# Fewer and larger transfers in the attention phase of a hybrid encoder layer

## The chip, the cores and the metric

The kernel runs on one core of one Trainium2 chip. The metric is the device time of one execution in microseconds (us). The kernel before was timed three times: 2056.21, 2058.32 and 2059.30 us, median 2058.32. About 0.2% (4 us) is what a measurement of this kernel can tell from no change.

## The reference

One layer over a prompt of 2048 frames and a sample of 32 new frames, width 1024, all in float32. One input projection gives, for every frame, q, k, v and a gate z of an attention branch A, q, k, v, a gate z and two small vectors of a delta-rule branch B, and two gates of 1024 columns each:

```python
qa, ka, va, za, qkv_b, zb, a_b, b_b, gate_a, gate_b = split_projection(x @ w_in)
oa = chunk_band_attention(qa, ka, va, rel_bias)        # 8 heads x 64, 9-chunk band of keys
ya = (oa.reshape(bsz, t, A_WIDTH) * jax.nn.silu(za)) @ w_branch_a
...                                                     # conv, gated delta rule in chunks of 64 -> ob
yb = (ob * jax.nn.silu(zb)) @ w_branch_b
mix = jax.nn.sigmoid(gate_a) * ya + jax.nn.sigmoid(gate_b) * yb
y = layer_norm(ALPHA * x + mix @ w_out, ln_g, ln_b)
```

The sample attends to 512 cached keys and values and to itself. Besides y, the layer returns the newest 512 rows of k and v, the last rows before the convolution and the final states.

## The kernel before

**Stages.** The 2048 frames are done in two halves of 1024 columns (the second with the 32 sample columns). For each half there is a branch-B stage and then a branch-A stage: B of half 0, A of half 0, B of half 1, A of half 1. A last stage, the merge, does the two branch products, the gates, the output product and the layer norm in eight blocks of 256 columns. Under all four stages one stream of projection jobs runs on PE (`multiply`, tile `pj` in PSUM, two banks): a job is a weight of 128 columns, split into an f16 high part `whi` and low part `wlo`, times the split input `hi`, `lo`, in column blocks of 512 or 272. Each finished product is read out of its bank by an `evac` stream, which then gives the bank back.

**Branch A.** The eight heads are four pairs `p`, two heads of 64 channels on the 128 partitions. For a pair, four jobs give v, k, q and z. K and Q are split into f16 parts too (`divide_rows`, line 1513) and must lie in layouts of their own: `kst` holds for head h its high part on its own 64 partitions and its low part on the other 64; `qd` holds the high part of head h on both halves; `ql` holds the low part on its own half, zeros on the other. So `divide_rows` writes both parts into a staging tile `part`, and DMAs carry 64-partition pieces from there into `kst`, `qd` and `ql` (lines 1683 and 1733). V's two parts go through `part` as well, and two transposing DMAs per 512 columns turn them into `vt` (line 1617). The scores of a tile of 128 queries are two products into `a`, then bias and maximum on DVE, the exponential on ACT, a split into `pu`, a transposing DMA into `pt`, and 15 products into `c` (line 1882). `store` (line 1907) fetches 64 KB of the gate z from DRAM into `ga`, transposes the result `ob` on PE, multiplies, and writes 64 KB of the gated result `g` back to DRAM. In half 1 the last 512 rows of k also leave through `kr` (line 1674, two buffers): an ACT read of the `pj` bank, PE transposes, ACT copies, DMAs to the output.

**Early products.** During A of half 1, branch B's results are already there, so its branch products (weights and `g` each in a high and a low part) are done early, as filling for PE (`early_g`, `early_sg`, `early`, line 2178 on): for each block of 256 columns and each of 8 row groups, 12 products into a `b` bank, a gate value tile `sge` loaded from DRAM, one DVE operation, a store of `sge` to DRAM. The g loads of successive blocks alternate between two places. The merge then loads these tiles again as `sg`.

**Order.** All of it is written by generators. A planner (`Flow`) gives each instruction and each DMA an assumed cost, and the stream with the earliest assumed clock emits next. The order in which instructions are emitted is then the fixed order of each engine's queue. Nearly all DMAs are issued from one queue, that of SyncE (SP): line 290 for plain ones, line 301 for transposing ones. An engine whose next instruction must wait holds up what stands behind it. `yield t` in a stream means "plan the next instruction not before t", where t is the assumed landing; `MARGIN` (1.6 us), `SLACK` (2.5 us) and `LEAD` are added to or taken from it.

Of the kernel before, what the change touches and what calls it, by code (L numbers as in the profile page):

```python
# [275 lines left out]
def trunk(ctx: ExitStack, tc: tile.TileContext, x_p, x_s, cache_k, cache_v, st_conv, st_gdn,  # L276
# [382 lines left out]

    def divide():  # L660

        while True:
# [8 lines left out]
            yield t  # L671
# [826 lines left out]
    def phase_a(half):  # L1498
# [8 lines left out]
        bias_slots, vs_slot, sample_slot = [gate(2), gate(1)], gate(2), gate(1)  # L1507
# [5 lines left out]
        def divide_rows(ps, m, leave):  # L1513

            i = yield from part_slots.take()
            hi, lo = parts[i][:, 0], parts[i][:, 1]
            S.activation(out=hi[:, 0:m], in_=ps[:, 0:m], func=AF.Copy, scale=SMALL)
            yield
            V.scalar_tensor_tensor(out=lo[:, 0:m], in0=ps[:, 0:m], scalar=SMALL, in1=hi[:, 0:m],
                                   op0=ALU.mult, op1=ALU.subtract)  # L1520
            yield from leave()
            return hi, lo, i
# [62 lines left out]
        def job_v(k):  # L1585
# [3 lines left out]
            def begin():  # L1589
                nonlocal vf, vt, t0  # L1590
                vf = ap.tile([P, KW + DEC], F32, tag="vf", bufs=1, name=f"vf{p}")
                k.vt = vt = ap.tile([P, 2, KW // P, P], F16, tag="vt", bufs=2, name=f"vt{p}")
                t0 = dma(vf[:, 0:BAND], v_dram[p][:]) if last else 0.0

            def rest():
# [10 lines left out]
                for t in range(0, KW // P, 4):  # L1606
# [45 lines left out]
        def job_k(k):  # L1652
# [10 lines left out]
            def evac(bi, c0, n, gcol, ps):  # L1663
# [36 lines left out]
        def job_q(k):  # L1700
# [18 lines left out]
            def evac(bi, c0, n, gcol, ps):  # L1719
# [18 lines left out]
                part_slots.back(place)  # L1738
# [52 lines left out]
        def scores():  # L1791
            before = mark()
            before.done()
            for k in pairs:
                for t in range(8 + SKEW):
                    for h, i in ((0, t), (1, t - SKEW)):
# [5 lines left out]
                        if h == 0:  # L1802
                            w = k.tiles[i] = Tile()
                            w.rs = sums[:, i + k.p % 2 * 8, :]
                            w.og, w.done = None, 0
# [60 lines left out]
        def product(h, k, t, gt, w, pu, place, nk, kc, at):  # L1866
# [12 lines left out]
            for i in range(nk):  # L1879
                kt = kc // P + i  # L1880
                oc = w.ps[:, h * HD:(h + 1) * HD]
                PE.matmul(oc, pt_[:, i], vt[:, 0, kt, hr], start=(i == 0), stop=False)
                PE.matmul(oc, pt_[:, i], vt[:, 1, kt, hr], start=False, stop=False)
                PE.matmul(oc, pt_[:, nk + i], vt[:, 0, kt, hr], start=False, stop=(i == nk - 1))
# [18 lines left out]
        NGA = 3  # L1903
# [649 lines left out]
```

## Time and profile before

| | us |
|---|---|
| median of three runs | 2058.32 |
| the profiled execution's own time | 2060.79 |
| its span, first to last instruction | 2059.0 |
| PE busy | 1920.5 (93%) |
| DVE busy | 1394.3 (68%) |
| ACT busy | 970.5 (47%) |
| GpSimd (POOL) busy | 806.0 (39%) |

The mean granted TensorE clock was 0.971. The page shows one execution. A busy PE is not PE at its peak: matmuls are pipelined, and a recorded matmul contains the wait for the one ahead of it. In the trace B of half 0 reaches to about 496 us, A of half 0 to about 815, B of half 1 to about 1280, A of half 1 to about 1735; the merge is in its steady form from about 1785 and the last block ends from 2014 on.

### The profile page before, as it was taken

The page shows a single profiled execution, that of the slowest core. Times are in us where ns is not written, and L with a number is a line of the kernel's source. Part 1 is how long each engine was busy: PE and PEld are TensorE (multiplying, and loading weights), DVE is VectorE, ACT ScalarE, POOL GpSimd, SP SyncE. Part 2 cuts the span into 40 slices and gives each one's busy share as a digit, 9 for nine tenths or more (in the row PEclk, how much of TensorE's full clock was granted, in tenths as well). Part 3 has the DMA queues.
Part 4 walks back from the last instruction along what each step waited for, and adds up shares of the span by engine and source line. Part 5 has one row for each costly group of instructions (what it writes and reads, how often), then busy time and mean ns, then how long its engine had stood idle before and what let it go on. Part 6 is the DMA issues. An engine that isn't in the chain of part 4 may idle for free.

```text
span 2059.0 us, 41305 instructions
## 1 busy us (share of the span) xinstructions
PE 1920.5 (93%) x14513; PEld 1350.5 (66%) x14513; DVE 1394.3 (68%) x4498; ACT 970.5 (47%) x1982; POOL 806.0 (39%) x1139
## 2 busy tenths in 40 slices
PE   8999999999998989999999999899998987799997
PEld 5455676665444556676777777577676765688885
DVE  7789989852457658589889884364454545675766
ACT  6655546444655766664445433454454544311110
POOL 7443334433333335344333423322221212455664
PEclk9999999999998999999999999999999998899998
DMA  3224232432577785223232333687778768634442
GB/s 139 65 76 125 74 98 66 112 91 95 135 183 170 173 190 136 76 71 96 68 86 65 98 95 91 163 200 162 182 164 207 168 167 200 212 125 152 143 132 76
DMA packets 398233, 263.91 MB, mean 128 GB/s; under 512 B 252994, under 2 KB 346542, under 8 KB 398024
## 3 DMA queue, kind: packets, MB, share of 16 engines
q1 hardware_dynamic: 398024, 261.26, 48.5%
q8 instruction: 114, 1.87, 0.4%
q14 instruction: 95, 0.78, 0.1%
HBM read 148.63 MB, written 63.24 MB: 103 GB/s over the span
## 4 chain that ended last, share of the span: by engine, by line
PE 59%; DVE 17%; DMA 6%; issue 6%; POOL 5%; ACT 4%; SPq 2%; POOLq 0%; DVEq 0%; ACTq 0%
PE pj L267 32%; PE b L267 13%; PE a L267 7%; PE x L267 3%; DVE acc L267 2%; DVE sys_t L267 2%; DVE sys_u L267 2%; POOL wlo L267 2%; PE c L267 2%; SPq L290 2%; PE o L267 2%; DMA pt<-pu 1%; DMA glo<-g 1%; DVE kd_bd L267 1%; ACT wraw L267 1%
## 5 line engine op out<-in xcount | busy, mean ns | idle before, releaser
L267 PE MATMUL pj<-hi,whi 128*128 128x512 f16 (+2 forms) x1992 | 649.8, 341 | 19.2 <-ACT whi L267 4.8
L267 PE MATMUL pj<-hi,wlo 128*128 128x512 f16 (+2 forms) x1952 | 641.5, 342 | 0.8 <-POOL wlo L267 0.7
L267 PEld LDWEIGHTS <-whi 128*128 128x128 f16 x3984 | 411.2, 105 | 232.6 <-issue 13.6
L267 PE MATMUL pj<-lo,whi 128*128 128x512 f16 (+2 forms) x1992 | 458.9, 340 | 0.0
L267 POOL TENSOR_TENSOR wlo<-wraw,whi 128x256 f16<-128x256 f32 x384 | 268.5, 722 | 441.6 <-ACT whi L267 334.5
L267 PEld LDWEIGHTS <-wlo 128*128 128x128 f16 x1952 | 206.3, 106 | 129.6 <-issue 20.4
L267 POOL TENSOR_TENSOR pu<-sb,pu 128x640 f16<-128x640 f32 (+2 forms) x64 | 82.7, 1292 | 208.8 <-ACT pu L267 177.9
L267 ACT ACTIVATE wraw<-wraw,w_scale 128x1024 f32<-128x1024 f32 (+1 forms) x98 | 111.4, 1137 | 90.7 <-DVE w_scale L267 80.1
L267 ACT ACTIVATE sb<-sb,mx,unit 128x640 f32<-128x640 f32 (+4 forms) x128 | 108.7, 850 | 83.4 <-DVE mx L267 80.0
L267 ACT CAST whi<-wraw 128x512 f16<-128x512 f32 (+1 forms) x196 | 119.0, 610 | 35.8 <-PE pj L267 33.0
L267 DVE TENSOR_TENSOR sys_u<-sys_u,sys_t 128x60 f32<-128x60 f32 (+24 forms) x527 | 124.8, 243 | 5.7
L267 ACT CAST mh<-sg 128x256 fp32r<-128x256 f32 x64 | 25.7, 406 | 210.5 <-DVE sg L267 187.7
L267 DVE SCALAR_TENSOR_TENSOR acc<-raw,cwT,acc 128x512 f32<-128x512 f32 x144 | 112.7, 783 | 7.9 <-ACT acc L267 6.5
L267 DVE TENSOR_TENSOR sys_t<-sys_u,sys_p 128x60 f32<-128x60 f32 (+21 forms) x459 | 109.9, 242 | 5.5
L267 POOL TENSOR_TENSOR w_scale<-w_scale,mhalf 128x1 f32<-128x1 f32 x49 | 30.6, 624 | 177.6 <-DVE w_scale L267 134.6
L267 DVE CUSTOM_DVE_ANT_0 sb<-a,bias 128x320 f32<-128x320 f32 (+5 forms) x136 | 66.2, 498 | 49.1 <-PE a L267 46.8
L267 PEld LDWEIGHTS <-pt 128*128 128x128 f16 x1680 | 66.7, 99 | 44.0 <-DMA pt<-pu 24.0
L267 ACT COPY v_t<-o 128x64 f32<-128x64 f32 x132 | 27.7, 210 | 142.8 <-PE o L267 99.5
L267 PE MATMUL c<-vt,pt 128*128 128x64 f16 x1680 | 72.1, 195 | 20.7 <-DMA pt<-pu 13.9
L267 DVE SCALAR_TENSOR_TENSOR sge<-sge,b 128x256 f32<-128x256 f32 (+1 forms) x64 | 27.1, 423 | 92.3 <-DMA sge<-sig 44.9
L267 ACT CAST pu<-sb 128x640 f16<-128x640 f32 (+4 forms) x128 | 81.9, 650 | 6.6 <-DMA pt<-pu 6.3
L267 ACT ACTIVATE sig<-pj,w_half 128x512 f32<-128x512 f32 (+2 forms) x84 | 49.3, 587 | 71.3 <-PE pj L267 63.6
(351 smaller groups left out, 4323.0 us busy)
## 6 DMA issues: line engine op xcount, KB each, us to landing
wraw<-in_w_in SPq DMA_DIRECT2D x192, 256.0 KB
sg<-sig SPq DMA_DIRECT2D x112, 128.0 KB
sig<-sig SPq DMA_DIRECT2D x44, 256.0 KB
sys_p<-sol_p SPq DMA_DIRECT2D x68, 128.0 KB
x<-in_x_p SPq DMA_DIRECT2D x16, 512.0 KB
xt<-in_x_p SPq DMA_DIRECT2D x16, 512.0 KB
out_y_p<-xt SPq DMA_DIRECT2D x16, 512.0 KB
glo<-g SPq DMA_DIRECT2D x14, 512.0 KB
```

What stands on the lines that cost most here:

```text
L267: r = f(*a, **k)
L290: eng.dma_start(dst, src)
```

## The change

- K and Q are split per head, straight out of PSUM: ACT writes the high part into its place in `kst` or `qd` (64 partitions at a time, so two instructions instead of one), DVE writes the low part of Q into `ql`, that of K into `part`. What is left for DMAs is K's low part, and a copy of Q's high part to the other half: 2 issues per block instead of 4 (K) and 6 (Q).
- V's two parts are turned by one transposing DMA instead of two, with a matching layout of `vt`.
- The gate is applied per two row tiles: loads and stores of 256 columns, one DVE operation; two places of two tiles instead of three of one.
- The early products of two 256-column blocks share one PSUM bank, one gate tile of 512 columns, one DVE operation, one load and one store (three such pairs; the last two blocks stay single). The products themselves stay 256 columns wide. A pair takes both places of the g loads. The gate tiles of early products and merge come from one pool of three, and the merge begins its loads when the early stream has ended.
- `kr` has one buffer instead of two.
- The planner assumes later landings: for weights (from the sixth job on), for the cached keys of the sample, for the early gate tiles (by 1.6 us ahead of the products, by 2.5 us ahead of the DVE operation).

The core of the diff:

```diff
-            yield t
+            yield t + (SLACK if len(started) > 4 else 0.0)
+            started.append(job)
...
-        bias_slots, vs_slot, sample_slot = [gate(2), gate(1)], gate(2), gate(1)
+        bias_slots, vs_slot, sample_slot = [gate(2), gate(1)], gate(1), gate(1)
...
-        def divide_rows(ps, m, leave):
-            i = yield from part_slots.take()
-            hi, lo = parts[i][:, 0], parts[i][:, 1]
-            S.activation(out=hi[:, 0:m], in_=ps[:, 0:m], func=AF.Copy, scale=SMALL)
+        def divide_rows(ps, m, his, los, leave):
+            for h in range(2):
+                S.activation(out=his[h], in_=ps[HS[h], 0:m], func=AF.Copy, scale=SMALL)
             yield
-            V.scalar_tensor_tensor(out=lo[:, 0:m], in0=ps[:, 0:m], scalar=SMALL, in1=hi[:, 0:m],
-                                   op0=ALU.mult, op1=ALU.subtract)
+            for h in range(2):
+                V.scalar_tensor_tensor(out=los[h], in0=ps[HS[h], 0:m], scalar=SMALL, in1=his[h],
+                                       op0=ALU.mult, op1=ALU.subtract)
             yield from leave()
...
-                        for i in range(2):
-                            at = turn(vt[:, i, t:t + 4, :], both[:, i])
-                        yield at
+                        yield turn(vt[:, t // 4].rearrange("p i k d -> p (i k) d"), both[:].rearrange("p i n -> p (i n)"))
...
-                        kr = ap.tile([P, 3 * P], F32, tag="kr", bufs=2, name="kr")
+                        kr = ap.tile([P, 3 * P], F32, tag="kr", bufs=1, name="kr")
...
-                hi, lo, place = yield from divide_rows(ps, m, leave)
+                place = yield from part_slots.take()
+                lo = parts[place][:, 0]
+                yield from divide_rows(ps, m, [kst[HS[h], h, cs] for h in range(2)],
+                                       [lo[HS[h], 0:m] for h in range(2)], leave)
                 for h in range(2):
-                    dma(kst[HS[h], h, cs], hi[HS[h], 0:m])
                     t = dma(kst[HS[1 - h], h, cs], lo[HS[h], 0:m])
...
-                hi, lo, place = yield from divide_rows(ps, m, leave)
+                yield from divide_rows(ps, m, [qd[HS[h], h, cs] for h in range(2)],
+                                       [ql[HS[h], h, cs] for h in range(2)], leave)
                 for h in range(2):
-                    for o in range(2):
-                        dma(qd[HS[o], h, cs], hi[HS[h], 0:m])
-                    t = dma(ql[HS[h], h, cs], lo[HS[h], 0:m])
+                    t = dma(qd[HS[1 - h], h, cs], qd[HS[h], h, cs])
...
-        NGA = 3
-        gas, obs = ([ap.tile([P, P], F32, name=f"{x}{i}") for i in range(NGA)] for x in ("ga", "ob"))
+        NGA = 2
+        gas, obs = ([ap.tile([P, 2, P], F32, name=f"{x}{i}") for i in range(NGA)] for x in ("ga", "ob"))
...
+            first.stored += 1
+            if first.stored == 2:
+                flow.start(leave_pair(k, t - t % 2, gt - t % 2, first.number))
+
+        def leave_pair(k, t, gt, place):
...
+            at = dma(ga[:].rearrange("p i n -> p (i n)"), za_dram[k.p][:, cs]) + SLACK
             yield at - LEAD / 4
             yield bank["b"]
             ps = pt("b")
-            PE.transpose(ps[:, 0:P], ob[:], ident[:])
+            for i in range(2):
+                PE.transpose(ps[:, i * P:(i + 1) * P], ob[:, i], ident[:])
             yield at
-            V.scalar_tensor_tensor(out=ga[:], in0=ps[:, 0:P], scalar=k.gsc[:], in1=ga[:], op0=ALU.mult, op1=ALU.mult)
+            V.scalar_tensor_tensor(out=ga[:].rearrange("p i n -> p (i n)"), in0=ps[:, 0:2 * P], scalar=k.gsc[:],
+                                   in1=ga[:].rearrange("p i n -> p (i n)"), op0=ALU.mult, op1=ALU.mult)
...
-            yield at
+            yield at + SLACK
...
-    sg_slots = [gate(SGB), gate(SGB)]
+    sg_slots, early_over = gate(SGB), mark()
+
+    def sg_tile():
+        return gp.tile([P, 2 * FW], F32, tag="sg", bufs=SGB, name="sg")
...
-        for b in range(NB):
-            if b in claimed_b or fp_open.at is not None:
+        for some in [[b, b + 1] for b in range(0, NB - 2, 2)] + [[NB - 2], [NB - 1]]:
+            if some[0] in claimed_b or fp_open.at is not None:
...
-                yield t - MARGIN
-                for m in g[2][0] + g[2][1]:
-                    yield m
+                yield t
+                for _, g, _ in what:
+                    for m in g[2][0] + g[2][1]:
+                        yield m
...
-                yield from branch(1, f, n, ps, g)
+                for i, ((_, g, _), m) in enumerate(zip(what, sizes)):
+                    yield from branch(1, f, m, ps[:, i * FB:], g)
...
-                    yield t
+                    yield t + SLACK
...
         yield fp_open
+        yield early_over
```

The order of all queues is planned anew. The numbers of DMAs on SP go from 1609 to 1357; PE has the same instructions in both kernels. Three places matter below.

**SP, first pair of A of half 0.** In the piece of the difference below, `vt`, `kst`, `qd` and `ql` are the layouts of V, K and Q, `part` the staging tiles, `wraw` a weight.

```order
-L301 DMA_TRANSPOSE vt_6085<-part_5980 128x4x128 x2
-L290 DMA kst_6168<-part_5981 64x512 x4
-L290 DMA wraw<-in_w_in 128x512 x2
-L290 DMA kst_6168<-part_5982 64x512 x4
-L290 DMA bias_6286<-ext_dram_95 128x640
-L290 DMA kst_d_102<-kst_6168 256x1x512
-L290 DMA qd_6264<-part_5979 64x512 x2
-L290 DMA ql_5983<-part_5979 64x512
-L290 DMA qd_6264<-part_5979 64x512 x2
-L290 DMA ql_5983<-part_5979 64x512
-L290 DMA wraw<-in_w_in 128x512 x2
```

```order
+L301 DMA_TRANSPOSE vt_6083<-part_5979 128x8x128
+L301 DMA_TRANSPOSE vt_6083<-part_5980 128x8x128
+L290 DMA kst_6165<-part_5981 64x512 x2
+L290 DMA wraw<-in_w_in 128x512 x2
+L290 DMA kst_6165<-part_5982 64x512 x2
+L290 DMA kst_d_102<-kst_6165 256x1x512
+L290 DMA bias_6284<-ext_dram_95 128x640
+L290 DMA qd_6260<-qd_6260 64x512 x2
+L290 DMA wraw<-in_w_in 128x512 x2
```

Between the V transposes and the second weight load stood 18 issues; now there are 10.

**ACT, first pair of A of half 1: the two writes of `kr`.** Before:

```order
L267 ACTIVATE kr<-pj,w_inv 128x272
L267 CAST whi_16136<-wr 128x512
L267 CAST whi_16138<-wr 128x512
L267 ACTIVATE part_16102<-vf_16196,vsc 128x512
L267 ACTIVATE part_16101<-pj 128x240
L267 ACTIVATE kr<-pj,w_inv 128x272
```

Now:

```order
L267 ACTIVATE kr<-pj,w_inv 128x272
L267 CAST whi_16044<-wr 128x512
L267 CAST whi_16046<-wr 128x512
L267 ACTIVATE part_16011<-vf_16107,vsc 128x512
L267 CAST whi_16044<-wr 128x512
L267 CAST whi_16046<-wr 128x512
L267 ACTIVATE kst_16218<-pj 64x240 x2
L267 COPY kr<-b 128x256
L267 COPY kr<-b 16x128
L267 ACTIVATE qd_16362<-pj 64x512 x2
L267 CAST whi_16044<-wr 128x512
L267 CAST whi_16046<-wr 128x512
```

The row that follows this last one is the second `kr<-pj,w_inv`. It has moved from ahead of the copies that empty the transposed rows into `kr` to behind them, and behind Q's first block.

**SP, the start of A of half 1: the loads `glo` of branch B's results for the early products.** Before:

```order
L290 DMA glo<-g_67 128x4x256
L290 DMA sig_72<-sig 128x272
L290 DMA bias_16178<-ext_dram_94 128x640
L290 DMA vf_16196<-v_d_106 128x512
L290 DMA wr<-in_w_b 128x1024
L290 DMA kst_16305<-kst_d_102 128x2x512
```

Now:

```order
L290 DMA glo<-g_67 128x4x256 x2
L290 DMA sig_72<-sig 128x272
L290 DMA bias_16089<-ext_dram_94 128x640
L290 DMA vf_16107<-v_d_106 128x512
L290 DMA wr<-in_w_b 128x1024
L290 DMA kst_16218<-kst_d_102 128x2x512
```

Both loads of the pair go first now; before, the second came 49 issues behind the first.

More of the change, by code (lines that the diff above doesn't have):

```diff
@@ L1909, in store @@
             yield
-            place = yield from ga_slots.take()
-            ga = gas[place]
-            for z, (c0, n, _) in zip(k.z, BLOCKS[half]):
-                if c0 < (t + 1) * P:
-                    yield z
-            at = dma(ga[:], za_dram[k.p][:, gt * P:(gt + 1) * P]) + SLACK
-            yield
-            ob = obs[place]
+            first = k.tiles[t - t % 2]
+            if first.place is None:
+                first.place = mark()
+                first.number = yield from ga_slots.take()
+                first.place.done()
+            yield first.place
+            ob = obs[first.number][:, t % 2]
             for h in range(2):
@@ L2208, in early @@
             if what is None:
+                early_over.done()
                 return
-            b, g, place = what
-            c0, n = b * FB, FB if b < NB - 1 else FW
-            q_eb.put(b)
+            sizes = [FB if b < NB - 1 else FW for b, _, _ in what]
+            c0, n = what[0][0] * FB, sum(sizes)
+            q_eb.put((c0, n))
             q_eg.low.give()
@@ L2268, in fold @@
             yield
-            sg_slots[1].give()
             yield m_slots[f]
```

65 lines of the change are left out of this document (38 added, 27 removed).

## The prediction

> **What bounds the kernel now.** I read the page's head first, then busy times by stage, then who waits for whom on PE within the stages, and last the queue of SP.
>
> The page's first line gives the span. The table by stage has, after the length, the busy times of PE, PEld, DVE, ACT and POOL with their counts, the granted clock, the busy share of the 16 DMA engines and GB/s.
>
> ```profile
> span 2059.0 us, 41305 instructions
> ```
>
> ```profile
> 30.00:496.00 466.00, 450.74 (x3218) 288.49 (x3217) 365.43 (x1297) 251.00 (x489) 193.18 (x315) 0.99 0.31 88
> 496.00:815.00 319.00, 293.51 (x2154) 163.79 (x2152) 195.73 (x700) 203.67 (x400) 125.84 (x160) 0.97 0.69 164
> 815.00:1280.00 465.00, 450.31 (x3797) 329.80 (x3795) 377.84 (x1311) 230.53 (x493) 176.02 (x314) 0.98 0.29 81
> 1280.00:1735.00 455.00, 418.50 (x3660) 310.49 (x3657) 219.98 (x738) 218.65 (x442) 116.21 (x128) 0.97 0.76 177
> 1735.00:1785.00 50.00, 25.98 (x155) 22.74 (x156) 32.18 (x55) 19.36 (x38) 20.02 (x16) 0.75 0.84 274
> ```
>
> PE bounds every stage but it idles unevenly: 25.5 us in A of half 0 (496 to 815), 36.5 us in A of half 1 (1280 to 1735), 24.0 us in the 50 us where the merge begins. The change touches the two A stages, so 62 us of idle time is what can be won there, and some clock with it. No other engine is full in them; the DMA engines are at 0.69 and 0.76, against some 0.3 in the B stages.
>
> The waits of PE in A of half 0, then in A of half 1 (total us, times, longest):
>
> ```profile
> PE c L267 <- DMA pt<-pu: 9.6, 9, 2.6
> PE c L267 <- DVE ob L267: 4.9, 2, 3.9
> ```
>
> ```profile
> PE b L267 <- DVE sge L267: 7.0, 4, 2.7
> PE a L267 <- DVE mx L267: 5.4, 2, 4.1
> PE b L267 <- DMA part<-in_cache_k: 5.2, 2, 2.8
> ...
> PE c L267 <- DMA pt<-pu: 2.8, 3, 2.0
> PE pj L267 <- ACT kr L267: 2.2, 2, 2.1
> ```
>
> Many of these end with a DMA that landed late: `pt`, the cached keys, and behind `sge` the gate loads. Why late? The queue of SP at the start of A of half 1 (start, us, what, count):
>
> ```profile
> 1321.76 1.11 SPq L290 DMA_DIRECT2D qd<-part  x2
> 1322.96 0.54 SPq L290 DMA_DIRECT2D ql<-part  x1
> 1323.55 1.24 SPq L290 DMA_DIRECT2D qd<-part  x2
> ...
> 1328.43 1.23 SPq L290 DMA_DIRECT2D qd<-part  x2
> 1329.70 0.59 SPq L290 DMA_DIRECT2D ql<-part  x1
> ...
> 1332.29 0.38 SPq L290 DMA_DIRECT2D glo<-g  x1
> ```
>
> SP issues for 10.5 us without a pause. Twelve of these issues are Q's layouts, and the load `glo` that early products wait for stands behind them. The chain of waits of this stretch goes through SP up to that load, and then through its landing:
>
> ```profile
> 1332.29 5.51 DMA glo<-g
> ```
>
> So in the A stages SP's queue is nearly a second bound: PE does not wait for SP's work as such, but for what stands behind it.
>
> **The change part by part.** Issue times (min/median/max ns) of what is removed:
>
> ```profile
> L290 SPq DMA_DIRECT2D kst<-part x80: 461/587/995, 524.6 to 1633.7; - x80
> L290 SPq DMA_DIRECT2D qd<-part x80: 467/588/1321, 532.9 to 1659.7; - x80
> L290 SPq DMA_DIRECT2D ql<-part x40: 462/594/1606, 534.4 to 1660.3; - x40
> L290 SPq DMA_DIRECT2D ga<-za x64: 319/448/1612, 567.6 to 1741.6; - x64
> L290 SPq DMA_DIRECT2D g<-ga x64: 319/404/1499, 579.8 to 1744.1; - x64
> L290 SPq DMA_DIRECT2D sge<-sig x64: 320/478/1557, 1331.8 to 1716.3; - x64
> L290 SPq DMA_DIRECT2D sig<-sge x64: 319/396/782, 1341.9 to 1720.3; - x64
> L301 SPq DMA_TRANSPOSE vt<-part x40: 1188/1217/2657, 518.4 to 1615.2; - x40
> ```
>
> K: 40 issues fewer, 23.5 us. Q: 40 of `qd` and 40 of `ql`, 47.3 us. V: 20 transposes fewer, 24.3 us. Gate: 32 loads and 32 stores, 14.3 and 12.9 us. Early tiles: 24 loads and 24 stores, 11.5 and 9.5 us. Sum 143 us of issue time, all within the two A stages (774 us). It is not a gain by itself, since SP is not what the end waits for; it takes SP away from the head of late transfers. I cost it by the waits above. Each is bounded below by nothing and above by its whole row:
>
> - Gate tiles of the early products (7.0): half the loads, and planned later by 1.6 and 2.5 us against a longest wait of 2.7. I take 5.
> - Cached keys (5.2): planned 2.5 us later, longest wait 2.8. I take 4.5.
> - `pt` (9.6 and 2.8): its own transposes stay, only what stands ahead of them on SP goes. Half, 6.
> - The rest of the 62 us, 37 us in many pieces (62 less the three rows' 24.6): those that come from late DMAs at the start of a pair (`kst`, `glo`, bias) shrink; those from ACT and DVE do not. A fifth, 7.5.
> - The clock. One late stretch in A of half 0, behind the loads of the second half's input, shows what idling costs besides:
>
> ```profile
> 618.00:640.00 22.00, 12.93 (x76) 6.72 (x76) 19.02 (x64) 12.44 (x24) 9.62 (x12) 0.61 0.91 199
> ```
>
> Granted 0.61 of full speed, 9.1 us idle. Over both A stages 0.97 of 774 us is 23 us of lost clock, a good half of it within idle time. If 23 of 62 idle us go, some 4 us of the other half follow.
>
> Gains together 27 us. Against that:
>
> - ACT and DVE do K's and Q's split in halves. The rows, with one of DVE that has 64 partitions:
>
> ```profile
> L267 ACT ACTIVATE part<-pj x40: 351/576/597, 521.9 to 1637.6; 128x512 f16<-128x512 f32 x24, 128x272 f16<-128x272 f32 x8, 128x240 f16<-128x240 f32 x8
> L267 DVE SCALAR_TENSOR_TENSOR part<-pj,part x40: 389/680/693, 522.7 to 1638.0; 128x512 f16<-128x512 f32 x24, 128x272 f16<-128x272 f32 x8, 128x240 f16<-128x240 f32 x8
> L267 DVE TENSOR_TENSOR q_bd<-qk,ex x32: 673/689/1216, 120.4 to 1179.2; 64x512 f32<-64x512 f32 x32
> ```
>
> 64 partitions of 512 columns take as long as 128, so each split costs twice: 23 us more on ACT, 27 on DVE over both stages. ACT and DVE are busy 422 and 416 of 774 us there, so this lies beside PE. But the `pj` bank is held 1.26 us longer, and DVE work queued behind waits. PE's rate for a 512-column job:
>
> ```profile
> 516.60 10.38 PE pj L267 x48
> ```
>
> 0.216 us a matmul, 24 to a product: 5.2 us, or 2.8 at 272 columns. A hold of 2.5 us fits under the product in the other bank. Without that cover it is 1.26 us for 40 splits, 50 us; I take 2.
> - The gate on DVE: 32 operations of 256 columns replace 64 of 128, and 24 early ones of 512 replace 48 of 256. Fewer, so no cost; DVE is not the bound. The PE transposes stay 64.
> - The pair takes both places of `glo`, so the next pair's g cannot be fetched while this one computes. A landing of 5.5 us, twice as much to bring, at three changes; projections and scores can cover it, but PE's order is fixed. From 0 to 3 x 5.5; I take 3.
> - The single `kr`: the chance of a stall on ACT and on a `pj` bank, priced below at 24 us if nothing covers it. I take a quarter, 6, since the planner knows of the one buffer and has put Q's product and early ones between.
> - Merge and B stages: unchanged instructions. The start of the merge waits for weights and `g` as before. 0.
>
> K and Q's removed DMAs move 64x512 f16 each, or 64 KB; in all 6.3 MB of some 133 MB that the table's rates give for the two A stages, under 5%. Gate and early transfers carry the same bytes as before. The Trainium skill, page "DMA: Bandwidth & Descriptors", section "Why small descriptors are slow (HBM only)", says that SBUF-to-SBUF transfers do not suffer from small pieces: by it, dropping K's and Q's copies frees SP's queue and hardly any bandwidth, and if bandwidth is what holds PE up, that part of the gain is nothing (rival 1). No row here measures a transfer of that kind alone.
>
> Sum: 2059.0 - 27 + 2 + 3 + 6 = 2043 by the span. The profiled execution took 2060.8, 1.8 more than its span and 2.5 more than the median, so some 2042 us as a median. The small pieces at the ends of a pair speak for rounding towards more gain, since SP's 143 us also shorten every K and Q; I say **2040**.
>
> **The rivals.**
>
> *1. The DMA engines, not SP, make transfers late.* They are at 0.76 where PE waits, and at 0.91 in its worst stretch. 5% fewer bytes leave that queueing as it is, and each removed issue only lets the next transfer wait further on. Only the later planning of cached keys and early tiles gains then (9), and the costs (11) stay: 2058 - 9 + 11 = 2060, or less where `kr` is covered; 2057. Against it: the queue of SP stood full for 10.5 us with `glo` behind it.
>
> *2. Slower: the one `kr` buffer.* The two writes of `kr` and the first output of it, in the first pair:
>
> ```profile
> 1306.11 0.49 ACT L267 ACTIVATE kr<-pj,w_inv 128x272 f32<-128x272 f32 x1 [0.51 <-DVE part L267]
> 1311.62 0.49 ACT L267 ACTIVATE kr<-pj,w_inv 128x272 f32<-128x272 f32 x1 [1.91 <-DVE part L267]
> 1320.80 0.90 SPq L290 DMA_DIRECT2D out_nk_p<-kr  x2
> ```
>
> The second write came 5.5 us behind the first. With one buffer it must wait until the output of the first has landed: 14.7 us to its issue, 0.9 for it, some 3 to land (an estimate, under the 5.5 of `glo`), so 13 us later. Until then K's last block keeps its `pj` bank, and PE has one bank: a product of 5.2 us, then 2.5 us of splitting in which PE waits, perhaps 6 us in 13. Behind the waiting write on ACT stand casts of weights, which PE waits for next. Four pairs, 24 us; with the gains halved by the same disorder, 2059 - 13 + 5 + 24 less 1: 2074. It decides from the point where scores, early products and the other bank fill less than half of the 13 us. For it: early products, the filling, are used up sooner now. Against it: SP being shorter, the output is issued sooner than 14.7 us.
>
> *3. Nearly all idle time of the A stages goes.* If SP was behind most of the 62 us, 45 go, and the clock gives 8: 2058 - 53 + 5 = 2010. Against it: the waits for `ob` and `mx`, 10.3 us (4.9 and 5.4), end on DVE, which gets more to do.
>
> **How the numbers follow.** Forecast (2026 to 2052): 0.48. Rival 1 (2050 to 2062): 0.17. Rival 2 (2062 to 2085): 0.18. Rival 3 (2005 to 2026): 0.17. The likeliest is 2040. Leaving out the far ends of rivals 2 and 3 gives 2011 to 2066. Faster by over 0.2% (under 2054): 0.47 of the forecast, all of rival 3, 0.06 of rival 1: 0.70. Within: 0.01, 0.08 and 0.02: 0.11. Slower: 0.19.
>
> **What would show it.** Right: PE's idle time in the A stages well under 62 us; the rows of PE waiting for `sge` and the cached keys nearly gone, `pt` halved; SP with pauses; the granted clock there above 0.97; ACT and DVE busy some 20 us more; the stages outside unchanged to a few us. Rival 1 shows as the same waits with SP idle between; rival 2 as ACT waiting for `out_nk_p` at `kr`, PE at `pj` for `kr`; the g changes as PE waiting for `ghi`. The forecast is wrong if the idle time only moves to the start of the merge, or if the new order brings waits of its own in B.

## The result: 2009 us, and the profile after

The changed kernel took 2009.46 us (median of four runs, 2002.91 to 2013.6), beside 2057.98 for the kernel before on the same chip: 0.976 of it, interval [0.973, 0.979]. Timed once more it was 2007.35 beside 2059.12, 0.975 [0.972, 0.977]. The gain is some 49 to 52 us. The prediction said 2040, a gain of 18, with 2011 as the lower end; the forecast itself is refuted, and what came is the time of rival 3.

The profiled execution of the changed kernel was the fastest of its four (2002.91 us), so its stages show 58 us and not 49. The head of its page, and the table by stage with the columns of the prediction (length, busy times of PE, PEld, DVE, ACT, POOL with counts, granted clock, share of the DMA engines, GB/s):

```profile
span 2001.1 us, 40919 instructions
...
PE 1903.8 (95%) x14513; PEld 1347.3 (67%) x14513; DVE 1410.8 (70%) x4482; ACT 993.7 (50%) x2022; POOL 807.2 (40%) x1139
```

```profile
30.00:497.00 467.00, 451.32 (x3219) 288.85 (x3218) 366.04 (x1298) 251.13 (x489) 193.19 (x316) 0.98 0.31 88
497.00:793.00 296.00, 286.31 (x2154) 162.22 (x2152) 202.29 (x700) 215.18 (x416) 129.05 (x160) 0.99 0.71 166
793.00:1255.00 462.00, 445.96 (x3797) 326.88 (x3795) 376.50 (x1311) 230.88 (x493) 176.31 (x314) 0.99 0.29 81
1255.00:1684.00 429.00, 408.94 (x3658) 307.71 (x3657) 232.70 (x724) 231.64 (x470) 117.35 (x130) 0.98 0.76 183
1684.00:1729.00 45.00, 30.31 (x164) 26.54 (x164) 31.79 (x56) 17.59 (x34) 19.61 (x17) 0.77 0.79 278
```

The stages are cut where PE has done the same number of matmuls as at the cuts of before. The A stages went from 319 to 296 and from 455 to 429 us, 49 in all. In them PE's idle time fell from 62.0 to 29.8 us, and PE's busy time, for the same matmuls, from 712.0 to 695.3. The start of the merge shrank by some 7 us (51.8 to 44.6, by PE's own count), although nothing in it was changed. The first B stage is as it was, the second 3 us shorter.

Who PE waits for in A of half 0, and in A of half 1 (total us, times, longest):

```profile
PE c L267 <- DVE ob L267: 2.5, 3, 1.2
PE b L267 <- DVE mx L267: 2.2, 1, 2.2
```

```profile
PE pj L267 <- ACT kr L267: 8.9, 2, 6.1
PE c L267 <- DMA pt<-pu: 4.6, 1, 4.6
PE c L267 <- DVE ob L267: 2.7, 3, 1.6
PE pj L267 <- DVE ql L267: 2.5, 1, 2.5
PE b L267 <- DVE sg L267: 0.5, 1, 0.5
```

The waits for `pt` of half 0 and for the cached keys are gone, that for the early tiles is at 0.5 of 7.0. Where did the waits go? Two stretches of SP's queue, the first of before at 587 us, where Q's layouts of the second pair are written (start, us, what, count):

```profile
587.75 1.40 SPq L301 DMA_TRANSPOSE pt<-pu  x1
589.21 1.45 SPq L290 DMA_DIRECT2D qd<-part  x2
590.75 0.54 SPq L290 DMA_DIRECT2D ql<-part  x1
591.34 1.23 SPq L290 DMA_DIRECT2D qd<-part  x2
592.62 1.61 SPq L290 DMA_DIRECT2D ql<-part  x1
594.33 1.01 SPq L290 DMA_DIRECT2D wraw<-in_w_in  x2
595.45 2.10 SPq L301 DMA_TRANSPOSE pt<-pu  x1
597.64 0.53 SPq L290 DMA_DIRECT2D bias<-ext_dram  x1
598.24 0.42 SPq L290 DMA_DIRECT2D ga<-za  x1
598.75 1.11 SPq L290 DMA_DIRECT2D qd<-part  x2
...
601.82 0.59 SPq L290 DMA_DIRECT2D ql<-part  x1
602.51 0.53 SPq L290 DMA_DIRECT2D g<-ga  x1
603.15 1.36 SPq L301 DMA_TRANSPOSE pt<-pu  x1
```

What is transposed at 603.15 is a `pu` that DVE had finished at 590.66, the first of these two:

```profile
L267 DVE TENSOR_TENSOR pu<-sb,pu x2: 811/818/824, 589.8 to 594.1; 128x640 f16<-128x640 f32 x2
```

It stood ready for 12.5 us, and Q's copies took some 7 of them. The same place in the changed kernel:

```profile
587.31 1.34 SPq L301 DMA_TRANSPOSE pt<-pu  x1
...
590.90 1.88 SPq L301 DMA_TRANSPOSE pt<-pu  x1
592.87 3.67 SPq L290 DMA_DIRECT2D qd<-qd  x2
596.64 1.35 SPq L301 DMA_TRANSPOSE pt<-pu  x1
```

```profile
L267 DVE TENSOR_TENSOR pu<-sb,pu x2: 815/820/826, 587.8 to 595.0; 128x640 f16<-128x640 f32 x2
```

Here the `pu` that DVE finished at 588.6 goes out at 590.90. For all 128 of these transposes, paired with the operations that write `pu` in order of time, I worked out from the traces how long each stood ready before its issue. The mean fell from 4.7 us in A of half 0 and 3.9 in A of half 1 to 0.85 and 0.66. For Q's 20 blocks, the time from the end of the split (its last operation on DVE) to the end of the last issue for the layouts fell from 12.6 to 1.6 us; counted from ACT's last write of the high part, which is all that the changed kernel's copies wait for, it is 3.2. SP's issue time in the two A stages, summed over its transfers, fell from 608 to 449 us.

One more transfer stood in that queue, `bias`, which DVE needs before it can begin on a head's scores. DVE waits for it in A of half 0 of before, in the changed kernel, and in the first experiment below, with 120 transfers added on SP:

```profile
DVE bias L267 <- DMA bias<-ext_dram: 11.4, 4, 5.3
```

```profile
DVE bias L267 <- DMA bias<-ext_dram: 2.9, 2, 1.6
```

```profile
DVE bias L267 <- DMA bias<-ext_dram: 11.1, 4, 4.8
```

### The profile page after: what moved, and what is told of

The parts are those of the page before. It is cut to its first block, busy times and chain, and to the rows that moved or that the text cites. A ratio compares the mean times of both kernels' runs of the same rounds, so it can differ in the third digit from the quotient of the medians.

```text
span 2001.1 us, 40919 instructions
## 1 busy us (share of the span) xinstructions
PE 1903.8 (95%) x14513; PEld 1347.3 (67%) x14513; DVE 1410.8 (70%) x4482; ACT 993.7 (50%) x2022; POOL 807.2 (40%) x1139
## 4 chain that ended last, share of the span: by engine, by line
PE 66%; DVE 19%; ACT 5%; issue 4%; POOL 2%; DMA 2%; SPq 1%; POOLq 0%; DVEq 0%; ACTq 0%
PE pj L267 38%; PE b L267 14%; PE a L267 7%; PE x L267 3%; DVE acc L267 2%; PE c L267 2%; DVE sys_t L267 2%; DVE sys_u L267 2%; PE o L267 2%; DVE kd_bd L267 1%; POOL wlo L267 1%; DVE q_bd L267 1%; ACT whi L267 1%; POOL xt L267 1%; DVE v_t L267 1%
## 5 line engine op out<-in xcount | busy, mean ns | idle before, releaser
L267 PE MATMUL a<-ghi,whi 128*128 128x256 f32 (+1 forms) x256 | 68.3, 296 | 12.8 <-ACT ghi L267 7.6
```

Of the source, the lines that this page charges most:

```text
L267: r = f(*a, **k)
```

## The experiments

Three theories went in. **A**: SP's issue time made the transfers late. **B**: the load of the copies on the DMA engines did. **C**: the new order of the work (early products used as filling sooner, later planned landings) filled PE's idle time. The column "SP" is its issue time in the A stages, "pt late" the mean wait of ready transposes in the two A stages, "Q late" the mean time from the end of Q's split to the end of the last issue for its layouts (negative where the copies of the high part go out before the low part is done), "bias" DVE's waits for the bias in both A stages, "idle" PE's idle time in the A stages, all from the one profiled execution of each, with stages cut by PE's count; the time is a median, and the last column is relative to the kernel before timed beside it.

| kernel | SP us | pt late us | Q late us | bias us | idle us | time us | of before |
|---|---|---|---|---|---|---|---|
| before | 608 | 4.7, 3.9 | 12.6 | 22.7 | 62 | 2058 | 1 |
| changed | 449 | 0.85, 0.66 | 1.6 | 5.9 | 30 | 2009.5, 2007.4 | 0.976, 0.975 |
| + 120 small on SP at K and Q | 525 | 2.0, 1.5 | 6.2 | 16.9 | 53 | 2038.6 | 0.990 [0.989, 0.992] |
| + 120 full-size on SP at K and Q | 518 | 2.0, 1.5 | 6.5 | 20.6 | 55 | 2040.6 | 0.991 [0.990, 0.993] |
| + 60 small on SP at K and Q | 484 | 1.4, 0.87 | 3.9 | 7.6 | 37 | 2017.5 | 0.981 [0.979, 0.982] |
| + 128 small on SP, spread | 532 | 2.5, 1.4 | 3.4 | 15.0 | 47 | 2028.9 | 0.986 [0.984, 0.988] |
| + 120 small on ACT at K and Q | 453 | 0.58, 0.72 | 1.8 | 3.3 | 37 | 2014.6 | 0.978 [0.976, 0.980] |
| K and Q undone | 534 | 2.3, 2.4 | 8.4 | 17.5 | 54 | 2046.3 | 0.993 [0.991, 0.996] |
| before, K and Q alone | 529 | 2.2, 2.2 | 6.3 | 10.2 | 40 | 2018.7 | 0.981 [0.979, 0.982] |
| V and gate undone | 504 | 2.2, 1.6 | 3.0 | 7.1 | 35 | 2019.4 | 0.980 [0.978, 0.983] |
| early pairs undone | 467 | 0.82, 1.1 | 1.8 | 4.8 | 30 | 2006.4 | 0.975 [0.972, 0.978] |
| planned landings undone | 441 | 0.69, 1.0 | 1.3 | 2.7 | 36 | 2012.0 | 0.978 [0.976, 0.980] |
| two `kr` buffers | 445 | 0.80, 0.92 | 2.1 | 4.1 | 30 | 2008.7 | 0.976 [0.973, 0.978] |
| Q's copies on ACT | 439 | 1.0, 0.87 | -0.5 | 1.8 | 27 | 2002.0 | 0.972 [0.970, 0.974] |
| Q's copies and more on ACT | 411 | 0.97, 0.74 | -0.5 | 2.3 | 42 | 2023.5 | 0.984 [0.982, 0.986] |
| Q's copies on ACT, casts later | 437 | 0.87, 0.94 | -0.6 | 0.9 | 26 | 2004.6 | 0.975 [0.973, 0.977] |

Neither SP's sum nor "pt late" orders the times: K and Q alone has `pt` later than + 120 small, at the same sum, and is 20 us faster. Among the kernels that issue from SP alone, the wait for `bias` comes nearest to ordering them. No run moves that load by itself, so it stands here as a sign, not as a shown cause.

### Transfers added to the changed kernel

Nothing is undone; transfers are added that nobody reads, without the planner knowing, so every other instruction stays in its place.

```diff
+    def spare(src):
+        i = len(extra)
+        extra.append(dram.tile([HD, src.shape[-1]], src.dtype, name=f"spare{i}"))
+        nc.sync.dma_start(extra[i][:], src)
...
                 for h in range(2):
+                    spare(mhalf[HS[h], :])
                     t = dma(kst[HS[1 - h], h, cs], lo[HS[h], 0:m])
...
                 for h in range(2):
+                    spare(mhalf[HS[h], :])
                     t = dma(qd[HS[1 - h], h, cs], qd[HS[h], h, cs])
+                    spare(mhalf[HS[h], :])
```

> The changed kernel with 120 transfers added on SP where the change took 120 out (two beside each K block's, four beside each Q block's), each of 64x8 f32 from a constant to a DRAM tile of its own that nobody reads; the planner is not told of them, so that no other instruction moves. They add SP issue time (120 by about 0.5 us, 60 of the 143 us that the change took away) and nearly no bytes (2 KB each). Theory A, SP's issue time made the transfers late: 60 / 143 of the 48 us come back, 2009 + 20 = about 2029, with PE's waits for pt, sg and the cached keys among the first again. Theory B, the DMA engines' load of copies: 2009, within 4. Theory C, the new order of the work (planner's later landings, early products used as filling sooner): 2009, within 4, too.

Measured 2038.64 us (2035.88 to 2040.88), 30 more than the changed kernel. Their issues, and the two A stages of this run:

```profile
L314 SPq DMA_DIRECT2D spare<-mhalf x120: 445/594/1890, 524.6 to 1647.6; - x120
```

```profile
496.00:804.00 308.00, 289.87 (x2152) 163.02 (x2150) 203.26 (x701) 215.08 (x416) 127.84 (x160) 0.98 0.68 160
...
1267.00:1718.00 451.00, 416.50 (x3660) 310.00 (x3659) 231.48 (x726) 231.75 (x470) 117.69 (x131) 0.97 0.73 175
```

2 KB each move next to nothing: GB/s is lower than in the changed kernel. Only SP's time is taken, and with it PE's idle time goes from 29.8 to 52.6 us and its busy time from 695.3 to 706.4. Of PE's waits, these in A of half 1, and then this one in A of half 0 (1.1 us in the changed kernel):

```profile
PE c L267 <- DMA pt<-pu: 10.7, 4, 5.0
...
PE b L267 <- DMA part<-in_cache_k: 2.5, 2, 1.7
```

```profile
PE a L267 <- DVE mx L267: 6.6, 5, 3.0
```

`pt` and the cached keys are back, as expected, the early tiles are not among the first; and a row that ends on DVE has grown, though DVE has no more work than before. DVE's own wait for `bias` grew with it, from 2.9 to 11.1 us in this stage. A stands, though 30 us came where it said 20, and C falls as the main cause: the order was the new one throughout.

The same with the size of the copies that the change removed (`spare(kst[HS[h], h, cs])`, and `qd` and `ql` for Q):

> The same 120 transfers beside the changed kernel's own, now with the size that K's and Q's removed copies had (64 rows of 512, 272 or 240 f16, from K's and Q's layouts to DRAM tiles that nobody reads), 6.3 MB in all. Theory A (SP's issue time): 70 of the 143 us are back, 2009 + 24 = 2033, and within 5 us of the run with small ones. Theory B (the load of the DMA engines): 2009 + 24 or more here, but 2009 with the small ones; the difference of the two runs is what the bytes cost. Theory C (order): 2009 in both.

Measured 2040.60 (2038.31 to 2042.95). 6 MB more cost 2 us, and the two intervals overlap: B falls. (The copies go to DRAM, the removed ones went to SBUF.)

Half as many, one beside each K block and two beside Q's:

> Half as many small added transfers on SP at the same places as in the first run with them: 60 in place of 120, one beside each K block's copies and two beside Q's. If the time lost is in proportion to SP's issue time: 2008 + 15 = 2023. If it starts at a load of the queue that the changed kernel stands well under: 2008 to 2014.

Measured 2017.45 (2015.26 to 2018.63), between the two forecasts: 9 us, for 35 of SP's time, where the other 60 cost 21 for 41. Relative to the kernel before, which ran 2 us faster beside this run, it is 11 and 19. A price that rises with SP's load fits this, a threshold not far above the changed kernel's load does too, and a plain proportion is hardly outside the spread; three points do not separate them.

At another place, one behind each transposition of `pt`:

> The changed kernel with 128 small added transfers (64x8 f32 to DRAM tiles that nobody reads) on SP again, but not where K and Q are written: one behind each of the 128 transposes of pt, which come evenly over the A stages. The planner is not told. Theory A1, SP's total issue time in the stage decides: 128 by 0.59 us is 76 us, at the 29 us that 71 us cost beside K and Q this is 31, 2040. Theory A2, only the bursts at K and Q decide (what stands behind them at the start of a pair is late): 2009 to 2020.

Measured 2028.86 (2028.59 to 2031.81), 20 us, between the two cases, and neither forecast holds: SP's time costs wherever it falls, 0.24 us for each here (20 for 83), and more where K's and Q's layouts are written, 0.40 (30 for 76). "Q late" goes with that: 3.4 us here and 6.2 with the transfers at K and Q.

On another queue, with `nc.scalar` in place of `nc.sync`:

> The same 120 small added transfers beside K's and Q's as in the first run with them, at the same places of the program, but issued from ACT and not from SP. If the time is SP's queue (theory A): 2009, plus what 71 us of issuing do to ACT, which is busy 444 of the 718 us of the A stages: 2009 to 2022. If it is the number of transfers in the DMA engines, whoever issues them: 2038 again.

Measured 2014.63 (2010.04 to 2015.46), 6 us in place of 30:

```profile
L314 ACTq DMA_DIRECT2D spare<-mhalf x120: 452/488/2060, 525.6 to 1627.3; - x120
```

The same transfers at the same places of the program, with the same bytes, cost a fifth when another engine issues them. It is SP's queue. The Trainium skill says in "DMA: Bandwidth & Descriptors", section "Issuing engines are not separate DMA queues", that starting transfers from several engines "will only save the time on the sequencer it takes to initiate the DMA, which is usually small relative to the DMA itself". The first half agrees; here the time on the sequencer was most of the effect, 24 of 30 us.

### Parts of the change, alone and undone

K's and Q's writes per head alone, in the kernel before (two `kr` buffers), and the other way round, the changed kernel with K and Q as before:

```diff
-                hi, lo, place = yield from divide_rows(ps, m, leave)
+                yield from divide_rows(ps, m, [qd[HS[h], h, cs] for h in range(2)],
+                                       [ql[HS[h], h, cs] for h in range(2)], leave)
                 for h in range(2):
-                    for o in range(2):
-                        dma(qd[HS[o], h, cs], hi[HS[h], 0:m])
-                    t = dma(ql[HS[h], h, cs], lo[HS[h], 0:m])
+                    t = dma(qd[HS[1 - h], h, cs], qd[HS[h], h, cs])
```

> The kernel before with K's and Q's writes per head alone: 120 issues fewer, 71 us of SP's time, 6.3 MB fewer; two kr buffers, gate, early products, V and the planned landings as before. Theory A: 71 / 143 of 48 us, 24: 2034. Theory B: the bytes of copies are all here, so most of the gain, 2015 to 2020. Theory C: the order of early products is the old one, so little: 2050 or more.

> The changed kernel with K's and Q's writes undone (split into a part buffer, three copies of Q and two of K per block as before); all else of the change stays, one kr buffer too. Theory A: 2009 + 24 = 2033. Theory B: most of the loss, 2045 or more. Theory C: 2015 or less.

Measured 2018.72 (2017.99 to 2023.69) and 2046.26 (2039.59 to 2050.65). K and Q alone give 40 of the 50 us, and without them 38 are lost. That is more than A's proportion of 24, and 8 us more than the 120 added transfers cost; both times lie where B put them. The bytes of B were tried only with copies to DRAM, so a part of B within these 8 us isn't excluded. The two kernels have the same issue time on SP (529 and 534) and are 28 us apart, so SP's sum alone doesn't set the time. They differ in what stands at K and Q, and in the planned order, which is new in each; the added transfers were in no plan at all. These were not separated, and what the 8 us are was not isolated; written per head, half of K's transfers and two thirds of Q's are not needed at all, which added transfers cannot bring back.

V's transposes and the gate's pairs undone together (the hunks on `vt`, `store` and `leave_pair`):

> The changed kernel with two parts undone: V's layouts by two transposes of half the size, and the gate per row tile (64 loads and stores of each kind). SP's issue time goes up by 24 + 27 = 51 us, evenly over the A stages. By the price of the evenly spread added transfers, 19 us for 76, that is 13 us: 2022. By the price of the bursts, 0.41: 2030. If K's and Q's bursts were all that counted: 2009 to 2013.

Measured 2019.41 (2014.19 to 2022.56), 11 us for 55 of SP's time: nearest to the price of the spread transfers.

The early products undone:

> The changed kernel with the early products undone: 256 columns at a time, one 256-column gate tile each, two pools of gate tiles, g in one place ahead, the planned landings of these tiles as before. 24 loads and 24 stores more, 21 us of SP's issue time. Theory A: 0.41 by 21 = 9, 2018. Theory C (the early products' new order is what filled PE's idle time in A of half 1): 2025 or more, with that stage's idle time back from 21 to 30 us or over. If fetching g for a pair at once costs what the prediction put down for it (3 us): 2015.

Measured 2006.43 (2002.26 to 2011.35), no difference from the changed kernel. Its wait for the early tiles is 3.4 us again, and costs nothing in the end. The order of the early products, theory C, gives nothing on top of the rest. A misses too: it said 2018, and 18 us more of SP's time in the A stages cost nothing at this load.

The planner's earlier landings back:

```diff
-                yield t
+                yield t - MARGIN
                 for _, g, _ in what:
...
-                    yield t + SLACK
+                    yield t
                     V.scalar_tensor_tensor(out=sg[:, 0:n], in0=sg[:, 0:n], scalar=1.0, in1=ps[:, 0:n],
```

(and `at` for `at + SLACK` at the cached keys, and the weights' `yield t`.)

> The changed kernel with the planner's earlier landings back: cached keys not planned later by 2.5 us, early gate tiles by 1.6 and 2.5 us earlier again, weights' landings as before. The prediction put these at 9.5 us of waits: 2008 + 9 = 2017, with PE waiting for sg and for the cached keys. If, with SP emptied, these loads land in time anyway: 2008, within 4.

Measured 2011.95 (2006.97 to 2017.51), some 4 us more with overlapping intervals: unclear. The row for the early tiles is 0.8 us and the cached keys have none, so with SP emptied these loads land in time.

### The kr buffer

```diff
-        NPART = 4
+        NPART = 3
-        bias_slots, vs_slot, sample_slot = [gate(2), gate(1)], gate(1), gate(1)
+        bias_slots, vs_slot, sample_slot = [gate(2), gate(1)], gate(2), gate(1)
-                        kr = ap.tile([P, 3 * P], F32, tag="kr", bufs=1, name="kr")
+                        kr = ap.tile([P, 3 * P], F32, tag="kr", bufs=2, name="kr")
```

> The changed kernel with two kr buffers again, paid for with three part buffers in place of four (Q needs none any more). If the single kr buffer costs what its rows show (8.9 us of PE waiting for ACT's kr, and half as much again in clock): 2009 - 13 = 1996. If those waits only hide others: 2009, within 4. If three part buffers hold up V and K: 2015 or more, with PE waiting for vf or the pj banks.

Measured 2008.71 (2004.94 to 2012.18): no difference. (The fourth `part` buffer given up for it could hide a small gain: PE's row for `part` is 1.7 us here and 0.3 in the changed kernel.) PE's row for `kr` stays with two buffers:

```profile
PE pj L267 <- ACT kr L267: 6.6, 2, 5.8
```

ACT's timeline shows why, first with two buffers, then in the changed kernel with one:

```profile
1297.72 1.14 ACT L267 CAST whi<-wr 128x512 fp32r<-128x512 f32 x2 [3.32 <-DMA wr<-in_w_b]
1298.88 0.49 ACT L267 ACTIVATE kr<-pj,w_inv 128x272 f32<-128x272 f32 x1
```

```profile
1293.92 1.14 ACT L267 CAST whi<-wr 128x512 fp32r<-128x512 f32 x2 [3.16 <-DMA wr<-in_w_b]
1295.52 0.49 ACT L267 ACTIVATE kr<-pj,w_inv 128x272 f32<-128x272 f32 x1 [0.46 <-DMA out_nk_p<-kr]
```

ACT stands 3.2 us at the cast of a weight whose load is under way, and the write of `kr` behind it; of the wait that the profile puts down to `kr`, the buffer's own share at this place is 0.46 us.

### Issuing from ACT

Since SP's issue time was the price, a version that beats both issues Q's remaining copies from ACT, behind the operations that write their source:

```diff
             for h in range(2):
                 S.activation(out=his[h], in_=ps[HS[h], 0:m], func=AF.Copy, scale=SMALL)
+            t = None
+            for h, to in enumerate(copies):
+                t = dma(to, his[h], nc.scalar)
             yield
```

> The changed kernel with Q's 40 copies into the other head's half issued from ACT, right behind the two ACT operations that write their source, in place of SP: same bytes, same number of transfers. SP loses 40 by 0.54 us = 22 us, ACT gets some 22 us of issuing more. Theory A (SP's issue time, 0.41 us of time for each us of it, from the runs with added transfers): 2009 - 9 = 2000. If ACT's in-order queue is what gets late (its casts of weights stand behind the copies): 2015 or more. If the number of transfers mattered and not who issues them: 2009, within 4.

> The changed kernel itself, timed anew beside the next one, since its four runs so far spread over 10 us. Every theory: 2009, within 4, 0.976 of the kernel before.

> The changed kernel with Q's 40 copies issued from ACT, once more, with five rounds on the same chip as the changed kernel. Theory A: 0.41 by 22 us, 9 us less than the changed kernel, 0.972 of the kernel before. If its first median of 2002 was a good draw: within 4 us of the changed kernel.

Measured 2001.91 (2000.89 to 2006.03), and beside the changed kernel 2002.02 (2000.31 to 2003.48) against 2007.35 (2002.92 to 2010.08): 0.972 [0.970, 0.974] of the kernel before. Some 5 us, in the direction of A, which said 9. SP's issue time in the A stages fell by 10 us and not by 22: the 40 copies took 26 us off it, and the issues of the `pt` transposes became 14 us longer.

More of the same, with the stores of the gates, of V's carried rows and of the new keys and values on ACT too:

> The run with Q's copies on ACT, and with more of SP's transfers on ACT: the stores of the gates to sig, of V's carried rows, and of the new keys and values, each right behind the ACT operation that wrote what it stores; some 80 issues more. If SP's issue time goes on paying in the A stages: 2002 - 4 = 1998. If the rest of the idle time has other causes, or ACT gets late: 2002 or more.

These are 112 transfers more on ACT in the trace, not some 80. Measured 2023.47 (2020.42 to 2029.45), 21 us more, with the least issue time on SP of all, 411 us. ACT's queue in A of half 1, and PE's wait:

```profile
1304.88 0.52 ACT L267 COPY kr<-b 128x256 f32<-128x256 f32 x2
1306.33 1.21 ACT L267 ACTIVATE qd<-pj 64x512 f16<-64x512 f32 x2 [0.94 <-PE pj L267]
1306.95 1.13 ACTq L290 DMA_DIRECT2D qd<-qd  x2
1308.13 1.30 ACTq L290 DMA_DIRECT2D out_nk_p<-kr  x2
...
1313.86 0.49 ACT L267 ACTIVATE kr<-pj,w_inv 128x272 f32<-128x272 f32 x1 [2.54 <-DMA out_nk_p<-kr]
```

```profile
PE pj L267 <- ACT kr L267: 13.9, 6, 3.9
```

Here the single `kr` buffer does cost: its output, copied by 1305.4, goes out only at 1308.1, behind Q's split and copies on ACT, and the next write waits 2.5 us for it. ACT releases `pj` banks, and what is queued on it in front of them is paid for by PE: this row is 13.9 us where it was 4.5. The rest of the 21 was not isolated.

Last, the weights' casts planned 4 us later, to take them away from in front of `kr` (`t + 4.0` for `t` in `split_w`, for the early products' weights):

> The run with Q's copies on ACT, with one kr buffer as in the changed kernel, and the casts of the early products' weights (whi from wr) planned 4 us later after their loads, so that they no longer stand ahead of the kr write on ACT while their load is under way. If that cast made PE wait at kr: its row (4.5 us there) goes to under 2 us with one buffer still, and the time is 2002 - 4 = 1998. If the single buffer makes it wait: the row stays, 2002. If the new order costs elsewhere: 2006 or more.

Measured 2004.63 (2001.34 to 2012.95), 0.975 [0.973, 0.977]. The row for `kr` is 4.8 us, as before the edit (4.5), and nothing is won. Which order would win this wait stays open.

## Why the prediction was wrong

**What bounds the kernel** was read rightly: SP's queue is nearly a second bound in the A stages, and what stands behind it is late. Added transfers on SP bring 30 us back, the same ones on ACT 6.

**The 143 us of issue time** came as 159 (608 to 449). The prediction then set this sum aside and costed by PE's own rows of waits. **That is the step that failed**, in three terms of the sum, against the one profiled execution:

- *Idle time.* Gross 23 us less 11 of costs, so net 12, was forecast; 32 went. The three named rows fell from 24.6 to 5.1 us, 19.5 where 15.5 was said. The rest, 37 us in pieces, of which I took a fifth, fell by 12.7 although the costs are within it. A row "PE waits for DVE `mx`" or "`ob`" ends on DVE, and I put it outside SP's reach; but with transfers added on SP the `mx` row of half 0 went from 1.1 to 6.6 us. DVE itself waits there for `bias`, which SP issues (11.1 us after 2.9); that `mx` came late by it is argued, not shown. The row names who came last, not who was late before him.
- *The costs of 11.* None of them shows as time. The single `kr` (6): with two buffers no difference, and at the place looked at 0.46 us. Both places of `glo` taken (3): undone, no difference. The split in halves (2): a wait for `ql` of 2.5 us, and K and Q as a whole are the gain. That the halves take as long as the whole was right, 0.59 and 0.68 us:

```profile
L267 ACT ACTIVATE qd<-pj x40: 360/591/593, 532.2 to 1610.2; 64x512 f16<-64x512 f32 x24, 64x272 f16<-64x272 f32 x8, 64x240 f16<-64x240 f32 x8
L267 DVE SCALAR_TENSOR_TENSOR ql<-pj,qd x40: 392/682/696, 533.4 to 1611.0; 64x512 f16<-64x512 f32 x24, 64x272 f16<-64x272 f32 x8, 64x240 f16<-64x240 f32 x8
```

- *The clock.* 4 us for 23 of idle time was forecast; PE's busy time for the same matmuls fell by 17 for 32. I had put a good half of the 23 us of lost clock inside idle time. By the clock in the traces 23.9 us were lost in the A stages of before, and 19.4 of them while PE was busy; in the changed kernel it is 6.8. So 13 of the 17 are clock, and the other 4 were not isolated. The last section shows what an idle piece costs behind it.

The start of the merge, put at 0, gave 7, and B of half 1 some 3, for which I have no cause; nothing was tried on them. With K and Q undone the start of the merge is as short (43.7 us), so it isn't those copies. 20 + 13 + 7 + 3 and the 16 of the sum are 59, beside the 58 of the two spans, of which the medians show 49 to 52.

**The early tiles and the cached keys**, 9.5 us of the forecast: their rows went as foreseen, but not by the parts I credited. Without the pairs the time is the same, and without the later landings the 4 us are within the spread. With SP's queue emptied, mostly by K and Q, these loads land in time.

**Rival 1** (the DMA engines) is refuted as the main cause: their share in the A stages is as high as before (0.71 and 0.76), and 6 MB more cost 2 us. **Rival 2** (the one `kr`) is refuted for this order, and its mechanism is seen where ACT issues the stores. **Rival 3** gave the time, 2010: it priced 45 us of idle time and 8 of clock, where 32 and 17 of busy time came, and 10 outside the A stages; that its sum fits is in part luck. What spoke against it, the waits that end on DVE, was the misreading above. It had 0.17.

## What to carry to other kernels

When one queue issues everything, look at how long a ready transfer stands in it before its issue, at what the engines ahead of PE wait for, and not only at whom PE waited for last. Price a removed issue by adding as many small ones beside it, with few bytes and with all of them, at another place, and on another queue; that separates issue time, bytes and place. A short queue elsewhere can take some of the issues, but only behind work of its own and not ahead of what releases a bank: 40 copies on ACT won 5 us, 112 more transfers lost 21.

## What was not expected of the hardware

A wait of PE shorter than three microseconds cost clock as well. Windows of 3.4 us in the kernel before, around PE's wait of 2.77 us for the cached keys in A of half 1:

```profile
1344.00:1347.40 3.40, 2.77 (x24) 2.13 (x22) 1.91 (x4) 3.06 (x7) 0.00 (x0) 1.00 0.79 244
1347.40:1350.80 3.40, 1.26 (x11) 1.17 (x12) 0.09 (x1) 1.26 (x4) 1.39 (x1) 1.00 0.98 313
1350.80:1354.20 3.40, 3.40 (x17) 2.89 (x17) 1.32 (x4) 0.79 (x2) 0.00 (x0) 0.50 1.10 264
1354.20:1357.60 3.40, 3.40 (x24) 2.28 (x21) 2.69 (x9) 0.65 (x2) 0.00 (x0) 1.00 1.15 202
```

PE was busy 1.26 of 3.4 us, and the whole next window ran at half clock, 1.7 us lost in work that waited for nothing. The Trainium skill, page "TensorE: Matmul & The Clock Gate", section "Part 1: The HAM clock gate", has the clock halved after an idle window of some 3.4 us. This trace agrees on the length and on the half, but the window need not be idle: in A of half 1 of this run the windows ahead of the seven stretches at half clock have 0 to 1.5 us of work in them. The clock in the traces changes at steps of 3.41 us. With the A stages of all 18 traces cut at these steps, of the windows at full clock that had under 1.3 us of work, 81 of 81 were followed by half clock; of those with 1.3 to 1.8 us, 15 of 49; of those with more, none of 3572. It is not the whole rule, since in B of half 1 of the same traces 34 of 2315 windows at full clock with over 2.2 us of work were followed by half clock too, for which nothing here shows a reason.

Over the A stages PE's busy time for the same matmuls moved by about half a microsecond for each of idle time: from before to the changed kernel 17 for 32, of which 13 are clock, and with 120 transfers added 11 for 23, of which 9 are.
